# A projection stage planned with other costs and in another order, and residual sums on VectorE

## The chip, the cores and the metric

The kernel runs on one core of a Trainium2 chip. A core has five engines, each with its own queue of instructions that is worked off in order: PE (TensorE, matrix products, with PEld its weight loads), DVE (VectorE), ACT (ScalarE), POOL (GpSimd) and SP, which here only issues DMA transfers. An instruction that waits for a semaphore holds up all that stands behind it on its engine. The metric is the device time of one execution in microseconds (us), lower is better; the kernel before takes 2375.2 us, the median of three runs (2374.72 to 2376.2).

## The reference

One layer of a backbone block over 2048 latent tokens and 256 context tokens of width 1024, all in fp32:

```python
hc = modulate(rms_norm(ctx, g_pre_mix), sm_c, cm_c)
_, _, xs_c, B_c, C_c, dt_c = mixer_inputs(hc, w_in, ...)          # context: x, B, dt (C unused)
_, hf_c, hb_c = ssd_bidir(xs_c, B_c, C_c, dt_c, ..., h0, h0)      # only the final states
hx = modulate(rms_norm(x, g_pre_mix), sm_x, cm_x)
u, z, xs, B, C, dt = mixer_inputs(hx, w_in, ...)                  # p = hx @ w_in; silu(conv7(x|B|C))
y, _, _ = ssd_bidir(xs, B, C, dt, ..., hf_c, hb_c)                # chunks of 128, both directions
x = x + gm_x * rms_norm(mixer_output(u, z, xs, y, ...), g_post_mix)
hx2 = modulate(rms_norm(x, g_pre_ffn), sf_x, cf_x)
x = x + gf_x * rms_norm((silu(hx2 @ w_gate) * (hx2 @ w_up)) @ w_down, g_post_ffn)
```

`w_in` has column groups u (Fourier, 256), z (768), x (768), B (512), C (512) and dt (24); the convolution runs over 7 taps within rows of 64 latent tokens, or over the 256 context tokens as one row. `mixer_output` adds a 2-D DFT of u and ends in a product with `w_out`.

## The kernel before

Each fp32 matrix is split into a high part `hi` (cast to fp32r) and the rest `lo` (a subtraction), and a product is three matmuls: hi·hi, hi·lo and lo·hi. A weight tile of 128 columns, `raw` (512 KB), is loaded by SP, cast to `hi` by ACT (or DVE), and `lo` is made by POOL or DVE (`split`, which finish_block starts with engines by its rule `brief`; G is POOL, V DVE, S ACT, T PE).

Time runs in this order in the profiled execution: to some 105 us norms and the first z blocks; to some 690 us the rest of the projection; then 16 chunks of scan outputs and `w_out` (to 1050), FFN gate and up (to 1950), and FFN down.

**The projection.** The tokens are three sections: 2 is the context (256 columns of a matmul's output), 0 and 1 are the halves of the latent (1024 columns, two PSUM banks). A block is (kind, j, section): 128 columns of `w_in` for one section, 48 matmuls of 512 columns for a latent block and 24 of 256 for a context block, into PSUM tiles `mm` (two) or `y` in turn. The list `blocks` gives their order. A block of x, B or C is convolved from PSUM into `acc`: ACT's first term, six DVE instructions (`acc<-mm,convw,acc`, 128x1008, 992 and 976 for two each, or 255, 254 and 253 for the context), ACT's silu, and PE's transposes (`a<-ident,acc`) to token rows through the two banks `a`. z and u blocks have no taps: call them light.

All engine calls of this stage go through `Paced`, one helper line (L143), which issues the call and charges its estimated cost to a model of time, `Pace`. Work behind a block is a chain (a generator); `Pace.due` lets a chain issue its next piece between two matmul groups once PE's model time has reached the chain's due time, so the estimates set where in each engine's queue a piece stands. `drain` forces a chain out at once: at the end of a block, finish_block drains the chains of the blocks before the last. Other chains are `scan_steps` of a section (POOL and DVE), the adaLN sums (`adacc`), and `section_chain(i)`, which loads half i of section 1's tokens (`load_rows`), normalises them (`xt`), and then, once `slot_free()` holds, transposes them (`a<-ident,xt`, 32 per half) and makes the modulated hi and lo in slot C or A (`v<-a,mcs` on ACT, casts and subtractions on DVE and POOL). Section 1 starts with u0 and u1: their first halves of columns, then a drain of section_chain(1), then the second halves.

**FFN down.** The order of engines and of SP's queue here comes from the program's order through a scheduler. Two passes p of 7 positions; each position has 11 steps f of 12 matmuls (`b<-wd,hd`), weights and hidden parts for which are prepared four steps ahead (`next_w`, `down_parts`): for each step ACT casts `wd` and `hd` and DVE subtracts for their lo parts, and for some positions the weight is first a difference of blocks (`wt`, or `actC` in place). A row group's end, `finish`, scales eight tiles on DVE (`slot<-slot,rq_y,gffn`), adds the residual to each (`slot<-slot,actC`), and issues one 2 MB output transfer (`out_dram<-slot`). It is a generator too, and advances `steps(run, 2)` per f of the next position.

Of the kernel before, what the change touches and what calls it, by code (L numbers as in the profile page):

```python
# [17 lines left out]
ALU = mybir.AluOpType  # L18
# [7 lines left out]
CTX = 256  # L26
# [106 lines left out]
class Paced:  # L133
# [5 lines left out]
    def __getattr__(self, op):  # L139
        issue = getattr(self.engine, op)  # L140

        def call(out, *args, **kw):
            r = issue(out, *args, **kw)  # L143
            n = math.prod(out.shape[1:])
            if self.name == "PE":
                fp32 = op == "matmul" and args[1].dtype == F32
                n = args[1].shape[-1] if op == "matmul" else 2 * P
                cost = max(n, 64) * (4 if fp32 else 1) / 2400
            elif self.name == "ACT":
                cost = 0.19 + n * 0.00075  # L150
                table = args[1] if op == "activation" and args[1] in (AF.Silu, AF.Exp, AF.Sigmoid, AF.Ln) else None
                if table not in (None, self.table):
                    self.table, cost = table, cost + 1.3
            elif self.name == "DVE":
                cost = 0.06 + n / (1920 if op in ("tensor_scalar", "tensor_copy") else 960)
            else:
                cost = 0.15 + n * 0.0021
            self.pace.charge(self.name, cost)
            return r

        return call
# [3 lines left out]
def fourier_ssd_block(ctx, tc, a):  # L165
# [624 lines left out]
    def group(kind, sec):  # L790
        return [(kind, j, sec) for j in range({"z": ZB, "u": 2, "x": XB, "B": BB, "C": CB}[kind])]

    c_, light = group("B", 2) + group("x", 2), group("z", 0)[4:] + group("u", 0)
    blocks = group("z", 0)[:4] + [("dt", 0, 2)]
    for i, blk in enumerate(light + group("B", 0)):
        blocks += c_[i : i + 1] + [blk]
    blocks += c_[8:]
    x_ = group("x", 0)
    blocks += x_[:5] + [("dt", 0, 0)] + x_[5:] + group("C", 0)
    u_, b_, x_, z_ = group("u", 1), group("B", 1), group("x", 1), group("z", 1)  # L800
    cl = group("C", 1)
    blocks += u_ + [("dt", 0, 1)] + b_ + x_
# [6 lines left out]

    wraw, wq = {}, {}  # L810

    def want(bi):
        if bi < len(blocks) and blocks[bi][0] != "dt":
            kind, j, sec = blocks[bi]
            c0 = off[kind] + j * P
            wraw[bi] = wload(w_in[:, :, c0 : c0 + P], [P, KD, P])

    def split(bi, *engines, **where):
        if bi in wraw:
            wq[bi] = wparts(wraw.pop(bi), [P, KD, P], *engines, **where)  # L820
        yield

# [115 lines left out]
    def down_parts(p, i, f):  # L938

        hpos[1] = (7 * p + i) * ((NJ + 1) // 2) + f // 2  # L940
        hidden_loads(3 if f % 2 == 0 else 2)

        def block(b):
            return wblock[p, (b, f // 4)][:, f % 4]

        def temp():
            return ta[0].tile([P, 512], F32, tag="ws", name="wt", bufs=4)

        def sub(engine, out, x, y):
            engine.tensor_tensor(out, x, y, op=ALU.subtract)  # L950
            return out

        i_ = ORDER[p][i]
        if i_ in (1, 5):
            src = block(11)
        elif i_ in (2, 3):
            src = block({2: 21, 3: 22}[i_])
        elif i_ == 6:
            sub(G, block(11), block(12), block(11))
            src = sub(V, temp(), block(22), block(11))  # L960
        elif i_ == 7:
            src = sub(G, temp(), block(22), block(12))
        else:
            src = sub(G, temp(), block(11), block(22))
            V.tensor_tensor(src, src, block(21), op=ALU.add)
        w = wp.tile([P, 2, 512], F32R, tag=("hi", "lo")[pos[1] % 2], name="wd")
        S.copy(w[:, 0], src)
        sub(V, w[:, 1], src, w[:, 0].bitcast(F32))
        raw = hraw[7 * p + i, f // 2][:, f % 2]
        tag, bufs = (("xt", 2), ("sg", 3))[pos[1] // 2 % 2]  # L970
        h = ta[0].tile([P, 2, 512], F32R, tag=tag, name="hd", bufs=bufs)
        S.copy(h[:, 0], raw)
        sub(V, h[:, 1], raw, h[:, 0].bitcast(F32))
        return w, h
# [427 lines left out]
    with tc.manual_schedule(engines=ordered):  # L1402
# [141 lines left out]
        def settled(kinds, sec):  # L1544
            return all(b in chains and chains[b].done for b in range(2, nblk) if blocks[b][0] in kinds and blocks[b][2] == sec)

        def finish_block(bi, ps):
            kind, j, sec = blocks[bi]
            live = [chains[b] for b in plain if b in chains and not chains[b].done and (blocks[b][2] == 2) == (sec == 2)]
            pace.drain(*live[:-1])  # L1550
            two = after(bi, 2)
            brief = two < nblk and any(blocks[b][2] == 2 for b in (after(bi, 1), two))
            splits[two] = pace.start(split(two, *((V, V) if brief and blocks[two][2] != 2 else (V,) if brief else (G,))))
            chains[bi] = pace.start(column_block(kind, j, sec, ps.rearrange("p a b -> p (a b)"), lambda: read.add(bi)))
# [11 lines left out]
        while bi < nblk:  # L1566
# [9 lines left out]
            want(after(bi, 2))  # L1576
            pace.drain(splits[bi])
            pace.now = max(pace.now, splits[bi].t)
            if (kind, j, sec) == ("x", 1, 0):
                prep1[0] = pace.start(section_chain(0, lambda: True))  # L1580
            if (kind, j, sec) == ("C", 0, 0):
                pace.drain(prep1[0])
                prep1[1] = pace.start(section_chain(1, lambda: 1 in begun))
            if bi == first1:
# [10 lines left out]
                    if i == 1:  # L1595
                        finish_block(b, pz[b - bi])
                fnet = pace.start(when(lambda: settled("u", 1), fourier_steps()))
                late.append(pace.start(when(lambda: fnet.done, load_wo(0, "B"))))
                bi += 2
                continue  # L1600
            if bi == plain[-3]:
# [15 lines left out]
                pace.drain(fnet, front, wts)  # L1617
                wo1 = load_wo(1, "C")
            if after(bi, 1) == first1:
                ps = project(bi, wq.pop(bi), acts[sec], lambda: begun.update({1: True}))  # L1620
            elif bi == plain[-1]:
                ps = project(bi, wq.pop(bi), acts[sec], beside=wo1)
            else:
                ps = project(bi, wq.pop(bi), acts[sec])
            finish_block(bi, ps)
            if kind == "x" and j == XB - 1:
                scan[sec] = pace.start(when(lambda sec=sec: settled("xB", sec), scan_steps(sec)), 8.0)
            bi += 1
        fourier_split(pend[0])
        pace.window = None  # L1630
# [219 lines left out]
    def finish(p, r, o, sq):  # L1850
# [6 lines left out]
        for t in range(4):  # L1857
            for n in range(2):
                oh = o[:, t, half[n]]
                V.scalar_tensor_tensor(oh, oh, rs[0][:, t : t + 1], gffn[n], ALU.mult, ALU.mult)  # L1860
                G.tensor_tensor(oh, oh, ff.x2[:, t, half[n]], op=ALU.add)
                yield
        b = PAIRS[p][r]
        dma(out_d[4 * b * P : 4 * (b + 1) * P, :].rearrange("(t p) d -> p t d", p=P), o)
# [42 lines left out]
    def down(p, prev):  # L1907
# [3 lines left out]
        for pos_, i in enumerate(order):  # L1911
# [9 lines left out]
            while f < NJ:  # L1921
# [7 lines left out]
                for ff_ in range(f, f + m):  # L1929
                    if (pos_, ff_) in at:  # L1930
                        down_load(*at[pos_, ff_])
                    steps(run, 2)
                    if (pos_, ff_) in rows:
                        rows_load(p, rows[pos_, ff_])
                f += m
# [64 lines left out]
```

## Time and profile before

| what | value |
|---|---|
| median of three runs | 2375.2 us (2374.72 to 2376.2) |
| the profiled execution: own time | 2376.4 us |
| its span, first to last instruction | 2374.6 us |
| busy: PE, DVE, ACT, POOL | 95%, 66%, 45%, 42% of the span |
| mean granted TensorE clock | 0.984 of full speed |

A share of busy time is an average over stages; a wait of PE is what can be won. Where a view names a releaser, it is what came last before the waiting instruction could start, by the profile. A granted clock of 0.5 is the lower of two levels, 1.2 in place of 2.4 GHz.

### The profile page before, as it was taken

To read this page: it belongs to the slowest core of one execution; us is meant where nothing else is said; L and a number is where in the kernel's file an instruction comes from. 1 tells how busy PE (TensorE), PEld (TensorE's weight loads), DVE (VectorE), ACT (ScalarE), POOL (GpSimd) and SP (SyncE) were. 2 spreads that over 40 slices of the span, in tenths; PEclk is the share of its full clock that TensorE was granted. 3 is DMA by queue.
4 is the path that set the end of the run, shared out by engine and by line. 5 is a ranking of instruction groups with operands and counts; after the bars stand their busy time and mean duration, and the time that the engine had idled before them with its cause. 6 is when DMAs were issued, how large, how long until landed. Compare 5 with 4: busy or idle time off the path is not lost. (4 is left out here: it accounts for less than half of the span.)

```text
span 2374.6 us, 30049 instructions
## 1 busy us (share of the span) xinstructions
PE 2261.2 (95%) x10861; PEld 1854.2 (78%) x10861; DVE 1557.1 (66%) x2202; ACT 1079.6 (45%) x1978; POOL 999.8 (42%) x659
## 2 busy tenths in 40 slices
PE   7998998999999999988999999999999999998998
PEld 3887777777788888866888887788888878876786
DVE  3557766567557888886655556755555565779766
ACT  4433553345247777756432323332333335444454
POOL 2121526424433444434555464445454532325512
PEclk9999999999999999999999999999999999999999
DMA  9455536354687888733332332433333373547233
GB/s 308 136 161 158 160 93 227 121 157 135 195 276 219 258 252 255 245 122 116 115 102 98 103 102 93 164 111 98 111 106 102 119 268 93 195 153 255 88 124 120
DMA packets 272291, 375.02 MB, mean 158 GB/s; under 512 B 17079, under 2 KB 190211, under 8 KB 269326
## 3 DMA queue, kind: packets, MB, share of 16 engines
q1 hardware_dynamic: 242486, 342.32, 45.3%
q10 hardware_dynamic: 29656, 30.78, 3.8%
q8 instruction: 86, 1.41, 0.2%
q14 instruction: 63, 0.52, 0.1%
HBM read 278.33 MB, written 94.72 MB: 157 GB/s over the span
## 5 line engine op out<-in xcount | busy, mean ns | idle before, releaser
L143 PE MATMUL b<-wd,hd 128*128 128x512 f32 x1848 | 429.2, 394 | 16.1 <-DVE hd L143 10.8
L143 PEld LDWEIGHTS b<-wd,hd 128*128 128x128 f32 x1848 | 349.9, 190 | 95.2 <-DVE hd L143 13.4
L143 PE MATMUL mm<-slot,wa 128*128 128x512 f32 x1584 | 378.4, 392 | 10.5 <-ACT sg L143 6.9
L143 PEld LDWEIGHTS mm<-slot,wa 128*128 128x128 f32 x1584 | 297.5, 189 | 75.6 <-ACT sg L143 7.7
L143 POOL TENSOR_TENSOR ws<-raw 128x512 f32<-128x512 f32 x88 | 127.4, 1449 | 311.8 <-DMA raw<-in_w_up_dram 117.7
L143 PE MATMUL mm<-actC,wa 128*128 128x512 f32 x984 | 239.8, 392 | 7.5 <-DVE u L143 7.2
L143 PE MATMUL mm<-actB,wa 128*128 128x512 f32 x1020 | 239.3, 389 | 0.0
L143 ACT CAST wa<-ws 128x512 fp32r<-128x512 f32 x176 | 109.2, 621 | 253.2 <-PE mm L143 213.4
L143 PEld LDWEIGHTS mm<-actC,wa 128*128 128x128 f32 x984 | 185.4, 189 | 47.2 <-issue 8.8
L143 PEld LDWEIGHTS mm<-actB,wa 128*128 128x128 f32 x1020 | 191.2, 188 | 39.6
L143 DVE TENSOR_TENSOR wa<-ws,wa 128x512 fp32r<-128x512 f32 x176 | 154.4, 879 | 59.6 <-ACT wa L143 56.7
L143 PE MATMUL mm<-actA,hi 128*128 128x512 f32 x512 | 165.9, 405 | 9.6 <-DVE acc L143 6.4
L143 DVE SCALAR_TENSOR_TENSOR acc<-mm,convw,acc 128x1008 f32<-128x1008 f32 (+3 forms) x156 | 161.9, 1040 | 19.5 <-ACT acc L143 16.5
L143 POOL TENSOR_TENSOR lo<-raw,hi 128x1024 fp32r<-128x1024 f32 x34 | 81.8, 2407 | 204.4 <-ACT hi L143 200.8
L143 DVE TENSOR_TENSOR u<-u,mm 128x512 f32<-128x512 f32 x126 | 86.5, 687 | 116.4 <-PE mm L143 116.3
L143 DVE TENSOR_TENSOR wa<-raw,wa 128x512 fp32r<-128x512 f32 x132 | 120.1, 911 | 64.5 <-ACT wa L143 64.0
L143 POOL TENSOR_TENSOR rq_y<-rq_ms,mhalf 128x1 f32<-128x1 f32 (+2 forms) x60 | 41.2, 691 | 284.3 <-DVE rq_ms L143 265.8
L143 ACT CAST wa<-raw 128x512 fp32r<-128x512 f32 x132 | 82.3, 624 | 161.9 <-PE mm L143 147.3
L143 POOL TENSOR_TENSOR adacc<-adacc,adaw 128x1024 f32<-128x1024 f32 x28 | 68.3, 2439 | 136.8 <-ACT adaw L143 136.8
L143 DVE TENSOR_TENSOR hd<-hraw,hd 128x512 fp32r<-128x512 f32 x154 | 117.3, 764 | 8.3 <-ACT hd L143 8.3
L143 PEld LDWEIGHTS mm<-actA,hi 128*128 128x128 f32 x512 | 95.1, 192 | 33.2 <-DVE acc L143 6.6
L143 ACT ACTIVATE ab<-ab,lda 128x128 f32<-128x128 f32 x384 | 118.8, 391 | 0.4 <-ACT sz L143 0.4
(309 smaller groups left out, 4534.6 us busy)
## 6 DMA issues: line engine op xcount, KB each, us to landing
hraw<-hg SPq DMA_DIRECT2D x70, 512.0 KB
raw<-in_w_in_dram SPq DMA_DIRECT2D x54, 512.0 KB
ab<-acsd SPq DMA_DIRECT2D x128, 192.0 KB
raw<-in_w_gate_dram SPq DMA_DIRECT2D x44, 512.0 KB
raw<-in_w_up_dram SPq DMA_DIRECT2D x44, 512.0 KB
hg<-hs SPq DMA_DIRECT2D x22, 1024.0 KB
adaw<-in_w_ada_dram SPq DMA_DIRECT2D x32, 512.0 KB
l_x<-xtok SPq DMA_DIRECT2D x33, 384.0 KB
```

The costliest lines, as they stand in the source:

```text
L143: r = issue(out, *args, **kw)
```

## The change

1. `Paced` charges a matmul 0.0135 us more, a DVE instruction 0.02 us more, and a tap of at least 256 elements 0.2 us in place of 0.06 beside its n/960.
2. `blocks`: each of the ten B and x tiles is now taken for the context and then at once for section 0, and the latent block uses the context block's hi and lo (`shared`): ten loads of 512 KB, ten casts and ten subtractions are gone. The six light blocks z4, z5, u0, u1 (those that are left) stand behind every second pair. Then C0, C1, dt, C2, C3. Before, context blocks alternated with light blocks and B0 of section 0, and x0 to x4, dt, x5 and C0 to C3 came behind them, each with its own weights.
3. section_chain(0) starts at the last x of section 0 (was x1), section_chain(1) at C3 (was C0). A scan also waits for its section's dt, and a latent scan for the context's scan. `load_wo(0)` also waits for the adaLN sums.
4. FFN down: the residual sums and, in the second pass, 11 weight subtractions go from POOL to DVE, and finish advances one step per f in place of two.

```diff
--- before.py
+++ after.py
@@ -145,14 +145,15 @@
             if self.name == "PE":
                 fp32 = op == "matmul" and args[1].dtype == F32
                 n = args[1].shape[-1] if op == "matmul" else 2 * P
-                cost = max(n, 64) * (4 if fp32 else 1) / 2400
+                cost = max(n, 64) * (4 if fp32 else 1) / 2400 + 0.0135
             elif self.name == "ACT":
                 cost = 0.19 + n * 0.00075
                 table = args[1] if op == "activation" and args[1] in (AF.Silu, AF.Exp, AF.Sigmoid, AF.Ln) else None
                 if table not in (None, self.table):
                     self.table, cost = table, cost + 1.3
             elif self.name == "DVE":
-                cost = 0.06 + n / (1920 if op in ("tensor_scalar", "tensor_copy") else 960)
+                taps = op == "scalar_tensor_tensor" and n >= CTX
+                cost = (0.2 if taps else 0.08) + n / (1920 if op in ("tensor_scalar", "tensor_copy") else 960)
             else:
                 cost = 0.15 + n * 0.0021
             self.pace.charge(self.name, cost)
@@ -790,13 +791,12 @@
     def group(kind, sec):
         return [(kind, j, sec) for j in range({"z": ZB, "u": 2, "x": XB, "B": BB, "C": CB}[kind])]
 
-    c_, light = group("B", 2) + group("x", 2), group("z", 0)[4:] + group("u", 0)
+
+    light, cl = group("z", 0)[4:] + group("u", 0), group("C", 0)
     blocks = group("z", 0)[:4] + [("dt", 0, 2)]
-    for i, blk in enumerate(light + group("B", 0)):
-        blocks += c_[i : i + 1] + [blk]
-    blocks += c_[8:]
-    x_ = group("x", 0)
-    blocks += x_[:5] + [("dt", 0, 0)] + x_[5:] + group("C", 0)
+    for i, (kind, j, _) in enumerate(group("B", 0) + group("x", 0)):
+        blocks += [(kind, j, 2), (kind, j, 0)] + (light[i // 2 : i // 2 + 1] if i % 2 else [])
+    blocks += cl[:2] + [("dt", 0, 0)] + cl[2:]
@@ -809,14 +809,19 @@
 
     wraw, wq = {}, {}
 
+    def shared(bi):
+        return bi > 0 and blocks[bi - 1][0] != "dt" and blocks[bi] == (*blocks[bi - 1][:2], 0) and blocks[bi - 1][2] == 2
+
     def want(bi):
-        if bi < len(blocks) and blocks[bi][0] != "dt":
+        if bi < len(blocks) and blocks[bi][0] != "dt" and not shared(bi):
             kind, j, sec = blocks[bi]
             c0 = off[kind] + j * P
             wraw[bi] = wload(w_in[:, :, c0 : c0 + P], [P, KD, P])
 
     def split(bi, *engines, **where):
-        if bi in wraw:
+        if bi < len(blocks) and shared(bi):
+            wq[bi] = wq[bi - 1]
+        elif bi in wraw:
             wq[bi] = wparts(wraw.pop(bi), [P, KD, P], *engines, **where)
         yield
 
@@ -956,7 +961,7 @@
         elif i_ in (2, 3):
             src = block({2: 21, 3: 22}[i_])
         elif i_ == 6:
-            sub(G, block(11), block(12), block(11))
+            sub(V if p else G, block(11), block(12), block(11))
             src = sub(V, temp(), block(22), block(11))
         elif i_ == 7:
             src = sub(G, temp(), block(22), block(12))
@@ -1544,6 +1549,10 @@
         def settled(kinds, sec):
             return all(b in chains and chains[b].done for b in range(2, nblk) if blocks[b][0] in kinds and blocks[b][2] == sec)
 
+        def ready_to_scan(sec):
+            dt_done = any(chains[b].done for b in chains if blocks[b] == ("dt", 0, sec))
+            return settled("xB", sec) and dt_done and (sec == 2 or scan[2].done)
+
         def finish_block(bi, ps):
             kind, j, sec = blocks[bi]
             live = [chains[b] for b in plain if b in chains and not chains[b].done and (blocks[b][2] == 2) == (sec == 2)]
@@ -1576,9 +1585,9 @@
             want(after(bi, 2))
             pace.drain(splits[bi])
             pace.now = max(pace.now, splits[bi].t)
-            if (kind, j, sec) == ("x", 1, 0):
+            if (kind, j, sec) == ("x", XB - 1, 0):
                 prep1[0] = pace.start(section_chain(0, lambda: True))
-            if (kind, j, sec) == ("C", 0, 0):
+            if (kind, j, sec) == ("C", CB - 1, 0):
                 pace.drain(prep1[0])
                 prep1[1] = pace.start(section_chain(1, lambda: 1 in begun))
@@ -1595,7 +1604,7 @@
                     if i == 1:
                         finish_block(b, pz[b - bi])
                 fnet = pace.start(when(lambda: settled("u", 1), fourier_steps()))
-                late.append(pace.start(when(lambda: fnet.done, load_wo(0, "B"))))
+                late.append(pace.start(when(lambda: fnet.done and ada.done, load_wo(0, "B"))))
                 bi += 2
                 continue
             if bi == plain[-3]:
@@ -1617,14 +1626,14 @@
                 pace.drain(fnet, front, wts)
                 wo1 = load_wo(1, "C")
...
             finish_block(bi, ps)
             if kind == "x" and j == XB - 1:
-                scan[sec] = pace.start(when(lambda sec=sec: settled("xB", sec), scan_steps(sec)), 8.0)
+                scan[sec] = pace.start(when(lambda sec=sec: ready_to_scan(sec), scan_steps(sec)), 8.0)
             bi += 1
         fourier_split(pend[0])
         pace.window = None
@@ -1858,7 +1867,7 @@
             for n in range(2):
                 oh = o[:, t, half[n]]
                 V.scalar_tensor_tensor(oh, oh, rs[0][:, t : t + 1], gffn[n], ALU.mult, ALU.mult)
-                G.tensor_tensor(oh, oh, ff.x2[:, t, half[n]], op=ALU.add)
+                V.tensor_tensor(oh, oh, ff.x2[:, t, half[n]], op=ALU.add)
                 yield
         b = PAIRS[p][r]
         dma(out_d[4 * b * P : 4 * (b + 1) * P, :].rearrange("(t p) d -> p t d", p=P), o)
@@ -1929,7 +1938,7 @@
                 for ff_ in range(f, f + m):
                     if (pos_, ff_) in at:
                         down_load(*at[pos_, ff_])
-                    steps(run, 2)
+                    steps(run, 1)
                     if (pos_, ff_) in rows:
                         rows_load(p, rows[pos_, ff_])
                 f += m
```

Three places show what moved in the engines' orders. The first is DVE in FFN down, at the start of the first `finish` (wd and hd are the lo parts of a step's weights and hidden part, slot is the row group that is finished, actC the residual's rows, rq_y the row factors). Before:

```order
L143 TENSOR_SCALAR rq_ms_16823<-fss_16821 128x4
L143 TENSOR_TENSOR wd_16829<-actB_15544,wd_16829 128x512
L143 SCALAR_TENSOR_TENSOR slot_16312<-slot_16312,rq_y_16825,gffn_15361 128x512
L143 SCALAR_TENSOR_TENSOR slot_16312<-slot_16312,rq_y_16825,gffn_15362 128x512
L143 TENSOR_TENSOR hd_16854<-hraw_16710,hd_16854 128x512
```

In the changed kernel:

```order
L143 TENSOR_SCALAR rq_ms_16763<-fss_16761 128x4
L143 TENSOR_TENSOR wd_16767<-actB_15484,wd_16767 128x512
L143 TENSOR_TENSOR hd_16790<-hraw_16650,hd_16790 128x512
L143 SCALAR_TENSOR_TENSOR slot_16252<-slot_16252,rq_y_16785,gffn_15301 128x512
L143 SCALAR_TENSOR_TENSOR slot_16252<-slot_16252,rq_y_16785,gffn_15302 128x512
L143 TENSOR_TENSOR slot_16252<-slot_16252,actC_16606 128x512
L143 TENSOR_TENSOR wd_16787<-actB_15484,wd_16787 128x512
```

The sums stood in POOL's queue, eight in a row; now each pair of a scaling and a sum stands between DVE's lo parts, and the sixteen instructions spread over more steps.

The second is DVE in the projection while a context block and a latent block are worked on (hi and lo are weight parts, acc the convolved block; 16x63 is a latent tap, 255 to 253 are context taps). Before:

```order
L143 SCALAR_TENSOR_TENSOR acc<-y,convw,acc 128x255 x2
L143 SCALAR_TENSOR_TENSOR acc<-y,convw,acc 128x254 x2
L143 CAST hi<-raw 128x1024
L143 TENSOR_TENSOR lo<-raw,hi 128x1024
L143 SCALAR_TENSOR_TENSOR acc<-y,convw,acc 128x253 x2
L143 SCALAR_TENSOR_TENSOR acc<-mm,convw,acc 128x16x63
L143 TENSOR_TENSOR lo<-raw,hi 128x1024
```

In the changed kernel:

```order
L143 SCALAR_TENSOR_TENSOR acc<-mm,convw,acc 128x255 x2
L143 SCALAR_TENSOR_TENSOR acc<-mm,convw,acc 128x254 x2
L143 SCALAR_TENSOR_TENSOR acc<-mm,convw,acc 128x253 x2
L143 TENSOR_TENSOR lo<-raw,hi 128x1024
L143 SCALAR_TENSOR_TENSOR acc<-mm,convw,acc 128x16x63 x2
L143 SCALAR_TENSOR_TENSOR acc<-mm,convw,acc 128x16x62 x2
L143 SCALAR_TENSOR_TENSOR acc<-mm,convw,acc 128x16x61 x2
```

The cast of a weight tile and one of the two subtractions are gone from between the taps, so that a latent block's taps stand in one piece.

The third is PE at the start of section 1 (xt are the normalised rows of a half, actC and actA its modulated parts, xd and l_b the scan's operands). Before:

```order
L143 MATMUL mm_3088<-actC_2214,lo_2928 128x512
L143 MATMUL a_3100<-ident_81,xt_2624 128x128
L143 MATMUL a_3100<-ident_81,xt_2626 128x128
L143 MATMUL a_3100<-ident_81,xt_2628 128x128
L143 MATMUL a_3100<-ident_81,xt_2630 128x128
L143 MATMUL mm_3088<-actC_2214,hi_2926 128x512
L143 MATMUL mm_3088<-actC_2215,hi_2926 128x512
```

In the changed kernel:

```order
L143 MATMUL a_3025<-ident_81,xt_2794 128x128
L143 MATMUL a_3025<-ident_81,xt_2796 128x128
L143 MATMUL a_3025<-ident_81,xt_2798 128x128
L143 MATMUL a_3025<-ident_81,xt_2800 128x128
L143 MATMUL a_3034<-xd_2996,l_b_2959 128x192 x2
L143 MATMUL a_3038<-xd_2996,l_b_2959 128x192 x2
L143 MATMUL a_3045<-ident_81,xt_2794 128x128
L143 MATMUL a_3045<-ident_81,xt_2796 128x128
L143 MATMUL a_3045<-ident_81,xt_2798 128x128
L143 MATMUL a_3045<-ident_81,xt_2800 128x128
```

Before, groups of four transposes stood between a C or u block's matmuls; now the 32 of the second half stand behind each other, with the scan's products as the only other rows among them, ahead of the second halves of u0 and u1.

## Rows read from the trace of the kernel before

**Rows 1.** The page's first part, busy time of the engines over the span.

```profile
PE 2261.2 (95%) x10861; PEld 1854.2 (78%) x10861; DVE 1557.1 (66%) x2202; ACT 1079.6 (45%) x1978; POOL 999.8 (42%) x659
```

**Rows 2.** The table of stretches: length, then busy time (and instructions) of PE, PE's weight loads, DVE, ACT and POOL, granted clock of TensorE (1.00 is the full 2.4 GHz), DMA share, GB/s.

```profile
200.00:250.00 50.00, 42.91 (x207) 34.70 (x206) 36.05 (x42) 19.06 (x30) 9.62 (x4) 0.93 0.46 136
300.00:350.00 50.00, 45.88 (x207) 35.36 (x206) 33.57 (x42) 26.39 (x34) 14.39 (x6) 0.93 0.24 68
350.00:400.00 50.00, 43.60 (x202) 34.85 (x201) 34.81 (x40) 19.08 (x22) 33.14 (x21) 0.90 0.78 255
450.00:500.00 50.00, 43.36 (x203) 35.85 (x202) 36.51 (x50) 26.27 (x37) 20.57 (x10) 0.97 0.40 118
2100.00:2170.00 70.00, 59.56 (x245) 46.98 (x244) 63.19 (x68) 28.36 (x57) 41.96 (x26) 0.95 0.50 174
2170.00:2350.00 180.00, 177.50 (x772) 145.50 (x771) 132.41 (x186) 82.65 (x156) 56.94 (x34) 0.99 0.43 140
```

**Rows 3.** Who waited for whom, PE in 100 to 700 us: us in total, times, longest. The first and the last of eleven rows and one between; all eleven add up to 38.3 us.

```profile
PE a L143 <- ACT acc L143: 8.6, 4, 4.0
...
PE mm L143 <- DVE lo L143: 0.6, 1, 0.6
...
PE a L143 <- POOL actC L143: 0.3, 1, 0.3
```

**Rows 4.** PE's timeline: start, length, instructions, and in brackets the idle time before and its releaser. The context pairs.

```profile
212.98 0.63 PE L143 MATMUL a<-ident,acc 128*128 128x128 f32 x4 [0.72 <-DVE br L143]
...
225.79 1.22 PE L143 MATMUL mm<-actA,hi 128*128 128x512 f32 x2 [6.37 <-DVE acc L143]
```

**Rows 5.** PE's timeline further on: four waits, and two rows of matmuls at the full clock behind the last of them.

```profile
269.47 1.12 PE L143 MATMUL a<-ident,xt 128*128 128x128 f32 x8 [2.37 <-DVE h L143]
...
330.96 1.14 PE L143 MATMUL a<-dtp,kc 128*128 128x96 f32 x4 [4.12 <-DVE dtp L143]
...
392.95 1.65 PE L143 MATMUL a<-xd,l_b 128*128 128x192 f32 x4 [6.35 <-ACT v L143]
...
490.60 1.70 PE L143 MATMUL a<-ident,acc 128*128 128x128 f32 x8 [4.01 <-ACT acc L143]
...
495.21 0.62 PE L143 MATMUL mm<-actC,hi 128*128 128x512 f32 x2
495.66 0.39 PE L143 MATMUL mm<-actC,lo 128*128 128x512 f32 x1
```

**Rows 6.** The table of stretches again (columns as in rows 2), two windows of 10 us.

```profile
170.00:180.00 10.00, 10.00 (x47) 8.31 (x46) 9.70 (x12) 2.66 (x4) 2.40 (x1) 1.00 0.60 164
220.00:230.00 10.00, 4.21 (x12) 3.43 (x13) 9.61 (x14) 2.85 (x4) 2.17 (x1) 0.73 0.61 176
```

**Rows 7.** PE in FFN down: two rows of who waited for whom (us, times, longest) in 1950 to 2374 us, and one of its timeline.

```profile
PE b L143 <- DVE hd L143: 10.1, 5, 4.0
PE b L143 <- DVE wd L143: 1.8, 1, 1.8
...
2127.46 27.79 PE L143 MATMUL b<-wd,hd 128*128 128x512 f32 x120 [1.67 <-DVE hd L143]
```

**Rows 8.** The timeline of DVE in FFN down, and one row of POOL's (the residual sums).

```profile
2119.23 1.78 DVE L143 TENSOR_TENSOR wd<-actB,wd 128x512 fp32r<-128x512 f32 x1
...
2122.63 1.40 DVE L143 SCALAR_TENSOR_TENSOR slot<-slot,rq_y,gffn 128x512 f32<-128x512 f32 x2
...
2127.93 0.68 DVE L143 TENSOR_TENSOR wd<-slot,wd 128x512 fp32r<-128x512 f32 x1
2128.53 0.68 DVE L143 TENSOR_TENSOR hd<-hraw,hd 128x512 fp32r<-128x512 f32 x1
...
2117.02 5.13 POOL L143 TENSOR_TENSOR slot<-slot,actC 128x512 f32<-128x512 f32 x3 [0.62 <-DVE slot L143]
```

**Rows 9.** The issue of an output transfer on SP's queue, and ACT's first evacuation of PSUM into a buffer of the same pool behind it.

```profile
2168.81 0.55 SPq L1864 DMA_DIRECT2D out_dram<-slot  x1
...
2177.71 0.59 ACT L143 COPY slot<-b 128x512 f32<-128x512 f32 x1 [0.27 <-PE b L143]
```

**Rows 10.** DVE's groups of instructions in 100 to 700 us, shapes apart: xcount, busy us, mean ns of one, idle before.

```profile
L143 DVE SCALAR_TENSOR_TENSOR acc<-mm,convw,acc 128x1008 f32<-128x1008 f32 x38 | 47.9, 1261 | 16.8 <-ACT acc L143 16.5
...
L143 DVE TENSOR_TENSOR lo<-raw,hi 128x1024 fp32r<-128x1024 f32 x16 | 21.6, 1351 | 10.2 <-ACT hi L143 9.3
...
L143 DVE CAST hi<-raw 128x1024 fp32r<-128x1024 f32 x8 | 9.2, 1150 | 24.7 <-PE mm L143 16.5 <-PE y L143 8.2
...
L143 DVE TENSOR_SCALAR xt<-xt,rq_y 128x1024 f32<-128x1024 f32 x8 | 7.6, 987 | 0.0
L143 DVE CAST actA<-v 128x512 fp32r<-128x512 f32 x8 | 6.8, 855 | 8.8 <-ACT v L143 8.8
L143 DVE SCALAR_TENSOR_TENSOR acc<-mm,convw,acc 128x254 f32<-128x254 f32 x14 | 6.7, 482 | 0.4
...
L143 DVE TENSOR_TENSOR actA<-v,actA 128x512 fp32r<-128x512 f32 x4 | 3.9, 981 | 0.2
```

**Rows 11.** The same view for ACT.

```profile
L143 ACT ACTIVATE acc<-acc 128x1024 f32<-128x1024 f32 x28 | 29.6, 1057 | 63.7 <-DVE acc L143 63.7
L143 ACT ACTIVATE acc<-mm,vcol,convw 128x1024 f32<-128x1024 f32 x19 | 22.8, 1202 | 2.4 <-PE mm L143 2.4
...
L143 ACT ACTIVATE v<-a,mcs 128x512 f32<-128x512 f32 x16 | 12.2, 777 | 20.3 <-PE a L143 17.5 <-POOL actA L143 1.9 <-DVE actA L143 0.7
```

More of the change, by code (lines that the diff above doesn't have):

```diff
@@ L1619, in fourier_ssd_block @@
             if after(bi, 1) == first1:
-                ps = project(bi, wq.pop(bi), acts[sec], lambda: begun.update({1: True}))
+                ps = project(bi, wq[bi], acts[sec], lambda: begun.update({1: True}))
             elif bi == plain[-1]:
-                ps = project(bi, wq.pop(bi), acts[sec], beside=wo1)
+                ps = project(bi, wq[bi], acts[sec], beside=wo1)
             else:
-                ps = project(bi, wq.pop(bi), acts[sec])
+                ps = project(bi, wq[bi], acts[sec])
             finish_block(bi, ps)
             if kind == "x" and j == XB - 1:
-                scan[sec] = pace.start(when(lambda sec=sec: settled("xB", sec), scan_steps(sec)), 8.0)
+                scan[sec] = pace.start(when(lambda sec=sec: ready_to_scan(sec), scan_steps(sec)), 8.0)
             bi += 1
```

## The prediction

> **What bounds the kernel now.** I read the page's engine totals first. PE is busy 2261.2 of 2374.6 us [rows 1], so all that any edit outside PE's own work can win is its 113.4 us of idle time and what a halved clock costs. In 700 to 1950 us the changed kernel has PE's instructions in the same order, one for one, and nearly all of the other engines' too; I take that part as unchanged. The table of stretches came next, for the rest [rows 2]. The change can act in 100 to 700 (the projection) and 2100 to 2350 (FFN down).
>
> In the projection the view of who waited for whom adds up to 38.3 us of PE waiting [rows 3]. The granted clock adds to it: a stretch of 50 us at 0.93 did 3.5 us less work than at 1.00, so 200–250, 300–350, 350–400 and 450–500 lost 3.5 + 3.5 + 5.0 + 1.5 = 13.5 us [rows 2]. Each of the four follows a long wait (6.37, 4.12, 6.35 and 4.01 us [rows 4, 5]): the matmuls right behind such a wait run at the lower of the two levels (two in 1.22 us at 225.79, against 0.62 at 495.21 [rows 4, 5]). A wait that goes takes its dip along. Together 51.8 us could come back.
>
> The waits differ by place. In 120–260 DVE is the limit: 9.70 of 10 us busy in 170–180, 9.61 in 220–230 while PE does 4.21 [rows 6]. Around the other waits DVE has 33 to 37 of 50 us [rows 2], and PE waits because a short instruction stood behind long ones in an in-order queue.
>
> In FFN down six waits, five on hd and one on wd, make 10.1 + 1.8 = 11.9 us [rows 7], and the clock adds 0.05 x 70 = 3.5 and 0.01 x 180 = 1.8 [rows 2]: 17.2. They coincide with the residual sums on POOL. DVE's subtraction of two SBUF operands starts every 0.60 us when POOL rests (2127.93, 2128.53), and takes 1.78 when a sum lies beside it (three sums in 5.13, 1.71 each) [rows 8]. So each sum costs DVE about 1.1 us. The Trainium skill ("SBUF — State Buffer", section "Who interferes with whom") says that a two-input VectorE instruction and a GpSimd one that reads SBUF exclude each other for a whole instruction; 1.78 against 0.60 agrees.
>
> **FFN down.** 24 sums leave POOL for DVE and 11 subtractions of the second pass too, and finish takes one step per f, not two. Per sum DVE loses a 1.1 us blockage and gains 0.60 us. Is there room? In the first of the places shown from the engines' orders, DVE's 28 rows from the first scaling to the last sum are 8 scalings at 0.66 (two in 1.40, the next begins 1.32 on [rows 8]) and 20 two-input rows at 0.60: 17.3 us. Six f's of PE are 6 x 2.78 = 16.7 (120 matmuls in 27.79 us, 12 per f [rows 7]). DVE falls back 0.6 us against a lead of up to three f's: no wait, but at full load. In the next finish 39 rows, 31 x 0.60 + 8 x 0.66 = 23.9 us, stand against nine f's, 25.0. The 11 moved subtractions make four two-input rows per f, 2.4 of 2.78. The out transfer now leaves near the end of a position, one position before its buffer gets new results from ACT; before, issue to that copy was 2168.8 to 2177.7 [rows 9], at most 8.9 us, against three prepared f's of 8.3. Against the move speaks the Trainium skill ("Perfetto Trace Analysis", section "Optimizing Scalar/DVE Operations"): when VectorE is saturated, offload work from it. By that rule this would lose; the same section warns that the two engines share a port, and the 1.78 us of the trace shows that here the offload itself costs more than the work. Bounds: 0 (blockage gone, DVE full instead) to 17.2. I take 13, nearer the top, since the load reaches 100% only in the first finish.
>
> **Context pairs (120–285).** Before, a pair of a context block and the next one cost DVE six taps of 1.25 (7.5), six of 0.48 (2.9), and for two weight tiles a cast of 1.15 and subtractions of 1.35 [rows 10]. With the latent block's cast and subtraction both there that is 7.5 + 2.9 + 2 x 1.35 + 1.15 = 14.2 against PE's 13.5: 48 x 0.225 = 10.8 (two matmuls begin 0.45 before the next, at 495.21 and 495.66 [rows 5]) and for the context 24 of half the columns, 2.7. DVE cannot keep up. Afterwards one tile serves both: 7.5 + 2.9 + 1.35 = 11.8, and behind every second pair stands a light block of 10.8 us of PE with no DVE work but a split. DVE's load is 2 x 11.8 + 1.35 = 24.9 of 2 x 13.5 + 10.8 = 37.8 us. The ten dropped loads, ACT casts and subtractions lie beside PE and give nothing else. What goes: 0.55 + 0.72 + 6.37 of waits [rows 3, 4] and 3.5 of clock: 11.1. What is late next is the transposes of a latent block, placed some 12 to 15 us behind its matmuls; six taps and two activations (7.5 + 1.2 + 1.1 [rows 10, 11]) need 9.8. Bounds 3 (the 6.37 halves only) to 11.1; I take 10.
>
> **C blocks, dt and the start of section 1 (285–410).** Here I expect a loss. Before: 2.37 + 0.33 + 4.12 + 6.35 = 13.2 of waits [rows 3, 5] and 8.5 of clock. Section_chain(0) starts four blocks later, so its 32 transposes share two PSUM banks with scan 2 in the one block C1: eight hand-overs of about 0.78 (one ACT evacuation [rows 11]), 6 us (bounds 2.7, as before, to 12). dt: 3.5 (3 to 4.1). Section_chain(1) starts at C3 where it started at C0; its 32 transposes now stand in one piece after u1's first half (the third of the places shown). PE waits there for the scaled rows (four times 0.99 on DVE [rows 10], behind taps), then for eight hand-overs of which its own 0.60 us transposes cover part: 9.5 (bounds 3.5, ACT's 8 x 0.78 less 8 x 0.60 and 2 for the rows, to 14). Dips 7.7 (5 to 9). Sum 26.7 against 21.7: −5, bounds +7 to −17.
>
> **Section 1 (410–690).** The rest of the 38.3 us, 38.3 − 7.6 − 13.2 = 17.5, and 1.5 of clock [rows 2, 3]. Before, taps were charged 0.06 + n/960 (1.11 us for 1008) where they take 1.26, and a matmul 0.213 where it takes 0.225; the planner's DVE thus ran about 1 us per block ahead of the real one, and a block's transposes went out at the block boundaries, in the forced drain. With 1.25 and 0.227 charged, they stand in mid-block with 3 to 5 us of slack by my sum of rows over PE's order. I keep 4 of waits, so 15 could go; bounds 0 to 19. I take 12, since scan and Fourier also move.
>
> **Sum.** −13 − 10 + 5 − 12 = −30 from the profiled execution's own 2376.4: 2346.4. The runs' median is 2375.2, 1.2 less: 2345.
>
> **Rivals.** (a) Everything found comes back: 17.2 + 11.1 + 15 and C to u1 as before, −43: 2332. For it: DVE has room on paper in each stretch. Against: hand-overs of two banks. (b) Only FFN down and the context pairs give; section 1's waits move to other places, C to u1 loses 5 to 10: −13 − 10 + 8 = −15: 2360. For it: ten separate small waits in section 1 with five different releasers, which better taps alone need not cure. (c) It does not do what it says: the planner's waits move, and DVE at full load in FFN down replaces the blockage: within 5 of 2375. Against: the 6.37 us has its own cause, removed. (d) Slower: the modulation of section 1's second half. It is one forced drain with nothing else for PE; each of eight groups goes transposes, ACT, cast, subtraction (0.60 + 0.78 + 0.86 + 0.98 = 3.2 us [rows 10, 11]), and if the groups go one after the other, behind the C blocks' taps on DVE (3 blocks of 7.5), it is 26 + 15 = 41 us, in place of 9.5, with a dip: +32 against −30 of the rest, 2380. It decides from 30 us of waiting at that place on. Against it: two banks and three engines overlap, and before the same chain cost 6.35.
>
> **How the numbers follow.** Forecast 0.52, own range 2336 to 2355; (a) 0.15; (b) 0.18; (c) 0.07; (d) 0.08. All lower bounds of time together give 17.2 + 11.1 + 7 + 19 = −54, all upper ones 0 − 3 + 17 − 0 = +14; neither is likely at once. Range for 8 in 10: 2327 (past (a)) to 2367 (past (b)). About 0.2%, 4.8 us, is what a measurement of this kernel can tell from no change. Faster by more: 0.52 + 0.15 + 0.18 and a little of (c), 0.87; within: 0.05; slower: 0.08.
>
> **What would show it.** FFN down: in 2100–2190 no DVE row of 1.7 us beside POOL and under 3 us of PE waits; wrong if DVE is 10.0 of 10 over 30 us with waits on wd or hd. Context pairs: no wait on acc over 2 us before 285 and DVE under 8.5 of 10. C to u1: one wait of 4 to 14 us before the second halves, releaser ACT v or DVE, and some on "a" banks in C1; over 30 us means (d). Section 1: waits on acc under 4 us in sum. The forecast as a whole is wrong if the clock dips are as many as before.

## The result, and the profile after

The changed kernel takes 2356.6 us (four runs, 2355.1 to 2359.9) against 2375.6, the median of four runs of the kernel before that were taken beside it: a ratio of 0.9922, 95% interval 0.9905 to 0.9939, some 19 us faster. The forecast was 2345, so −30. The profiled execution is the slowest of the four, with a span of 2358.1 us.

Where the 19 us come from is seen by the starts of two late stages. The rows are PE's first matmuls of FFN gate and of FFN down, first in the kernel before:

```profile
1036.45 2.88 PE L143 MATMUL mm<-slot,wa 128*128 128x512 f32 x12
...
1919.62 8.32 PE L143 MATMUL b<-wd,hd 128*128 128x512 f32 x36
```

and in the changed kernel:

```profile
1035.78 2.88 PE L143 MATMUL mm<-slot,wa 128*128 128x512 f32 x12
...
1921.25 8.32 PE L143 MATMUL b<-wd,hd 128*128 128x512 f32 x36
```

Gate starts 0.7 us earlier, down 1.6 us later. FFN down to the span's end took 2374.6 − 1919.6 = 455.0 us before and 2358.1 − 1921.3 = 436.8 after: 18.2 us less. All that lies ahead of it won nothing that two profiles can tell apart (the experiments show how far such starts scatter). The table of stretches (columns as in rows 2) shows that this nothing is a sum. Before:

```profile
100.00:285.00 185.00, 174.66 (x908) 146.79 (x908) 126.55 (x166) 75.11 (x103) 48.23 (x24) 0.98 0.51 152
285.00:410.00 125.00, 114.47 (x526) 91.14 (x525) 87.68 (x102) 52.16 (x63) 55.99 (x32) 0.93 0.52 165
410.00:700.00 290.00, 272.45 (x1348) 224.45 (x1348) 180.60 (x248) 120.98 (x169) 121.00 (x61) 0.99 0.57 181
```

After:

```profile
100.00:285.00 185.00, 184.73 (x954) 155.65 (x954) 106.89 (x134) 75.10 (x97) 40.87 (x17) 1.00 0.45 134
285.00:410.00 125.00, 105.32 (x465) 80.86 (x464) 81.47 (x108) 54.71 (x71) 52.10 (x30) 0.89 0.43 136
410.00:700.00 290.00, 275.38 (x1370) 228.14 (x1369) 189.85 (x254) 121.51 (x167) 130.29 (x67) 0.98 0.58 187
2100.00:2180.00 80.00, 80.00 (x353) 65.95 (x352) 74.79 (x126) 40.37 (x78) 3.72 (x3) 1.00 0.70 241
```

In 100 to 285 PE goes from 174.66 to 184.73 us of 185 at the full clock; [rows 4] have no counterpart left. In 285 to 410 it loses: 114.47 to 105.32, and the clock falls from 0.93 to 0.89. In 410 to 700 it gains 3 us of busy time and loses 0.01 of clock on 290. Over the three together PE is busy 565.4 us in place of 561.6, but the low clock costs 13.8 + 5.8 = 19.6 us (the part lacking to 1.00 times the length, stretch by stretch) where it cost 3.7 + 8.8 + 2.9 = 15.4. In 2100 to 2180 the waits of [rows 7] are gone, 80.00 of 80. Who waited for whom, PE in 100 to 700 us, shows what stands there in place of [rows 3]:

```profile
PE a L143 <- DVE h L143: 13.8, 2, 10.2
PE a L143 <- ACT v L143: 4.6, 4, 2.4
PE a L143 <- DVE dtp L143: 4.2, 1, 4.2
...
PE a L143 <- ACT acc L143: 1.0, 1, 1.0
```

All eleven rows add up to 34.1 us where [rows 3] had 38.3. The waits on acc have shrunk from 8.6 us to 1.0; one on `h`, the scan's state, is the longest now.

DVE's timeline in the first finish answers to [rows 8]:

```profile
2111.80 1.41 DVE L143 SCALAR_TENSOR_TENSOR slot<-slot,rq_y,gffn 128x512 f32<-128x512 f32 x2
2113.12 0.68 DVE L143 TENSOR_TENSOR slot<-slot,actC 128x512 f32<-128x512 f32 x1
2113.72 0.68 DVE L143 TENSOR_TENSOR wd<-actB,wd 128x512 fp32r<-128x512 f32 x1
2114.33 0.68 DVE L143 TENSOR_TENSOR slot<-slot,actC 128x512 f32<-128x512 f32 x1
```

Sums (`slot<-slot,actC`) and lo parts start 0.60 us apart, and none takes 1.78. In the second finish DVE has no idle time over 20 us, and PE (first column) does not wait. The kernel before has DVE at 10.00 of 10 in both windows too, but with 9 and 7 rows done where there are now 18 and 17, and PE busy for 5.93 and 5.99 us:

```profile
2150.00:2160.00 10.00, 10.00 (x46) 8.29 (x45) 10.00 (x18) 4.53 (x8) 0.00 (x0) 1.00 0.64 197
2160.00:2170.00 10.00, 10.00 (x45) 8.29 (x45) 10.00 (x17) 5.79 (x12) 0.00 (x0) 1.00 0.63 220
```

### The profile page after: what moved, and what is told of

Its sections match the earlier page's. It is cut to its first block, busy times and chain, and to the rows that moved or that the text cites. A ratio compares the mean times of both kernels' runs of the same rounds, so it can differ in the third digit from the quotient of the medians.

```text
span 2358.1 us, 29985 instructions
## 1 busy us (share of the span) xinstructions
PE 2261.0 (96%) x10861; PEld 1855.0 (79%) x10861; DVE 1531.9 (65%) x2220; ACT 1082.5 (46%) x1979; POOL 943.3 (40%) x623
## 5 line engine op out<-in xcount | busy, mean ns | idle before, releaser
L143 PE MATMUL b<-wd,hd 128*128 128x512 f32 x1848 | 423.0, 391 | 4.2 <-ACT hd L143 2.0
L143 DVE TENSOR_TENSOR hd<-hraw,hd 128x512 fp32r<-128x512 f32 x154 | 109.9, 714 | 5.7 <-ACT hd L143 5.6
```

## The experiments

All are timed beside the kernel before on the same chip (medians of 2374.8 to 2375.4 us); ratios are to it. The first four are about FFN down and the sum of the two halves of the change, the others about the projection. A profile of one run has its limits here: before, e1, e3 and e4 have the same instructions ahead of FFN down, and their first gate matmul starts at 1036.5, 1034.2, 1033.4 and 1035.7 us; the changed kernel and e2, which share theirs, have 1035.8 and 1033.8. Differences of 3 us between two profiles of that part are not read.

**e1_down_only.** The kernel before with part 4 of the change:

```diff
-                G.tensor_tensor(oh, oh, ff.x2[:, t, half[n]], op=ALU.add)
+                V.tensor_tensor(oh, oh, ff.x2[:, t, half[n]], op=ALU.add)
-                    steps(run, 2)
+                    steps(run, 1)
-            sub(G, block(11), block(12), block(11))
+            sub(V if p else G, block(11), block(12), block(11))
```

> The kernel before with part 4 of the change alone (sums and the second pass's subtractions on DVE, finish one step per f). Theory one, FFN down gives all of the gain: 2357 to 2359 us, the waits on hd and wd in FFN down under 3 us in sum, the projection as before. Theory two, the gain needs both halves of the change: 2366 or more.

Measured: 2357.0 us, 0.9931 (0.9916 to 0.9946). Who waited for whom, PE in 1950 to 2374 us, has for `b` only this left:

```profile
PE b L143 <- DVE slot L143: 1.4, 3, 0.7
```

Theory one: this part alone gives 18.0 us, nearly as much as the whole change's 19.

**e2_proj_only.** The changed kernel with the three edits above undone.

> The changed kernel with part 4 undone: new costs, order, sharing and chain starts, FFN down as before. Theory one (context pairs win some 12 us, the start of section 1 and the blocks behind it give all of it back): 2373 to 2376 us, FFN down with 11 to 12 us of waits on hd and wd again. Theory two: 2366 or less, the projection gives half of the gain.

Measured: 2377.0 us, 1.0007 (0.9998 to 1.0016), a little above the range named. The projection's edits as they stand are worth nothing, and the same view shows FFN down's waits as in [rows 7]:

```profile
PE b L143 <- DVE hd L143: 9.7, 5, 3.5
PE b L143 <- DVE wd L143: 1.8, 2, 1.5
```

**e3_sums_fast** has only the first of the three edits, **e4_steps_only** only the second.

> The kernel before with the residual sums on DVE, but two steps of finish per f and the subtractions on POOL. If the engine of the sums is what counts: 2358 to 2362 us. If the slower pace of finish is needed too, since DVE then has 4 of 6 two-input rows per f too many (about 3.6 us of DVE work per f of 2.78): 2364 to 2370, with waits of PE on hd and wd of 5 to 8 us left.

> The kernel before with one step of finish per f and the sums still on POOL. If the blockage itself is the cause, spreading halves its density and most of the lost DVE time is caught up by the three prepared steps: 2360 to 2366 us. If each blockage costs PE time whatever its spacing: 2372 to 2376.

Measured: e3 2361.8 us, 0.9951 (0.9934 to 0.9967); e4 2371.2 us, 0.9987 (0.9977 to 0.9996). The engine of the sums brings 13.1 us, the rest of part 4 another 4.8 (by medians; the intervals of e1 and e3 overlap). In e3 two waits in the second finish are left (PE's timeline), where two steps per f ask DVE for more than a step's time (by the estimate above, 3.6 us of 2.78):

```profile
2153.83 3.01 PE L143 MATMUL b<-wd,hd 128*128 128x512 f32 x12 [1.71 <-DVE hd L143]
2158.59 6.64 PE L143 MATMUL b<-wd,hd 128*128 128x512 f32 x28 [1.75 <-DVE hd L143]
```

In e4 the waits remain at nearly their size, though the sums are spread out (who waited for whom, PE in 1950 to 2374 us):

```profile
PE b L143 <- DVE hd L143: 5.3, 3, 2.3
PE b L143 <- DVE wd L143: 4.0, 1, 4.0
```

e4 lies between its two cases and nearer to the second: spacing gives 3.7 us, the blockage by POOL is what costs. Whether the slower pace or the moved subtractions bring e1's last 4.8 us was not tried apart.

**e5_prep_early** starts section_chain(1) one block sooner.

```diff
-            if (kind, j, sec) == ("C", CB - 1, 0):
+            if (kind, j, sec) == ("C", CB - 2, 0):
```

> The changed kernel (2356.6 us) with section_chain(1) started at C2 in place of C3. Theory one, its rows come too late (PE waits on xt, 2.33 and 0.34 us at 385 us, and the four waits behind them): those on xt go, 2350 to 2354 us. Rival, the hand-overs of the two banks in the drained piece are the price, whenever the rows are there: 2355 to 2358.

Measured: 2359.4 us, 0.9932 (0.9918 to 0.9947). The waits on xt went, but others stand in PE's timeline, one of them on POOL's weight split. The first and the last row are the start of u0 and of its second half:

```profile
369.52 0.61 PE L143 MATMUL mm<-actC,hi 128*128 128x512 f32 x2
...
377.79 0.50 PE L143 MATMUL mm<-actC,lo 128*128 128x512 f32 x1 [1.70 <-POOL lo L143]
...
388.19 1.58 PE L143 MATMUL a<-ident,xt 128*128 128x128 f32 x8 [1.97 <-ACT v L143]
391.90 1.62 PE L143 MATMUL a<-xd,l_b 128*128 128x192 f32 x4 [2.14 <-issue]
...
396.39 1.20 PE L143 MATMUL mm<-actA,hi 128*128 128x512 f32 x2
```

By time this is the rival's case, and 1 us above it; by mechanism it is neither. The stretch from the start of u0 to that of its second half is shorter, 26.9 us (396.39 − 369.52) where the changed kernel takes 33.8 (its rows stand below), and its waits are 7.1 us in place of 8.8. The gain is lost behind it: in 410 to 700 PE is busy 271.6 us where it was 275.4, and gate starts at 1036.1.

**e6_old_costs** and **e8_no_sharing** take the new estimates, or the sharing, out of the changed kernel.

```diff
-        return bi > 0 and blocks[bi - 1][0] != "dt" and ...
+        return False and bi > 0 and blocks[bi - 1][0] != "dt" and ...
```

> The changed kernel with the estimates of the kernel before, order and sharing kept. If the new estimates are worth something: 2360 to 2367 us, with waits on acc back in section 1 (410 to 700 us). If they are worth nothing in this order: 2354 to 2359.

> The changed kernel with a load and a split of its own for every block, order kept. If sharing is what removes the wait on DVE in the context pairs (14.2 us of DVE work against 13.5 of PE per pair without it): 2361 to 2368 us with waits on acc or lo before 300 us. If the light blocks between the pairs give room enough: 2355 to 2359 and no such wait.

Measured: e6 2352.3 us, 0.9906 (0.9891 to 0.9921); e8 2349.2 us, 0.9890 (0.9875 to 0.9904). Both are faster than the changed kernel, which neither theory had. In e6 the waits on acc are back, as forecast, with 7.4 us in 410 to 700, and still it is 4.3 us faster. In e8 every block splits its own weights again, and yet (the table of stretches, 100 to 285 and 170 to 180 us):

```profile
100.00:285.00 185.00, 184.73 (x955) 155.84 (x954) 124.94 (x157) 76.53 (x99) 40.66 (x17) 1.00 0.53 156
170.00:180.00 10.00, 10.00 (x57) 8.75 (x56) 7.61 (x7) 2.93 (x3) 2.41 (x1) 1.00 0.80 243
```

PE waits for nothing there, with DVE at 7.61 of 10 where [rows 6] have 9.70. Sharing is not what removed the wait of 6.37 us, and the new estimates are not either: f2 below, with neither, is busy 184.39 of 185 there, and f3, with the new estimates in the old order, keeps a wait of 6.51 on acc at 226.23. It is the order; that the light blocks between the pairs give DVE the room is the reading that fits.

**e7_fourier_after_scan** holds one chain back.

```diff
-                fnet = pace.start(when(lambda: settled("u", 1), fourier_steps()))
+                fnet = pace.start(when(lambda: settled("u", 1) and scan[0].done, fourier_steps()))
```

> The changed kernel with the Fourier chain held until the scan of section 0 is done. Theory one, PE's wait of 10.16 us at 478 us is the scan's h addition standing on DVE behind Fourier's pieces (5.58 us for four of them beside POOL): it goes with the low clock behind it, 2343 to 2350 us. Rival, DVE is full there in any order (scan, taps and dt together) and the wait only moves: 2354 to 2360.

Measured: 2355.5 us, 0.9920 (0.9903 to 0.9936), the rival's range. PE's wait of 10.16 us is gone from the trace, so that Fourier stood in the way holds; but PE's timeline has a new one close by, for section 1's dt:

```profile
449.02 1.14 PE L143 MATMUL a<-dtp,kc 128*128 128x96 f32 x4 [5.50 <-DVE dtp L143]
```

In DVE's timeline ahead of it, seven short pieces of dt take 8.61 us; another takes 0.36 at 447.07, when POOL rests:

```profile
438.26 8.61 DVE L143 SCALAR_TENSOR_TENSOR dtp<-dtp 128x192 f32<-128x192 f32 x7
```

In that time POOL runs four rows with two inputs each, from 437.51 to 445.48 without a gap.

**f1_noshare_fourier** is e7 and e8 in one, **f2_order_alone** is e6 and e8 in one, **f4_noshare_fourier_old** all three. **f3_costs_down** is e1 with the new estimates: the old order, no sharing.

> The changed kernel without sharing and with the Fourier chain held until section 0's scan is done, both edits together. If each removes a wait of its own (sharing: the start of section 1; Fourier: the wait behind the scan at 450 to 490 us): 2341 to 2346 us. If both only draw another arrangement of the same queue pieces, their gains don't add: 2347 to 2356.

> The changed kernel without sharing and with the old estimates: of the projection's edits the order, the chain starts and the scan's conditions alone. If order is what gives in the projection, and estimates and sharing nothing: 2346 to 2353 us, PE without a wait from 100 to 300 us. If sharing or estimates were needed for it: 2356 or more.

> The kernel before with part 4 (2357.0 us without more) and the new estimates, old order and no sharing. If the estimates mend the waits of section 1, as forecast: 2342 to 2350 us. If they only move them: 2353 to 2361.

> No sharing, Fourier held, old estimates, with the changed order and part 4. If the old estimates gain 4 us in any arrangement, as they seemed to in the first: 2338 to 2344 us. If estimates only draw another arrangement: 2345 to 2354.

Measured, with the other kernels that have part 4:

| order | sharing | Fourier held | old estimates | new estimates |
|---|---|---|---|---|
| old | no | no | e1: 2357.0 | f3: 2347.0, 0.9882 (0.9869 to 0.9896) |
| new | no | no | f2: 2363.9, 0.9955 (0.9942 to 0.9967) | e8: 2349.2 |
| new | no | yes | f4: 2351.1, 0.9900 (0.9886 to 0.9913) | f1: 2343.9, 0.9872 (0.9857 to 0.9887) |
| new | yes | no | e6: 2352.3 | the changed kernel: 2356.6 |
| new | yes | yes | not run | e7: 2355.5 |

The new estimates are worth 10.0, 14.7 and 7.2 us in the first three rows, and cost 4.3 in the fourth. Sharing gains 11.6 us with the old estimates and loses 7.4 with the new (11.6 with Fourier held). The new order with its chain starts and scan conditions alone loses 6.9 us, or 2.2 with the new estimates. Holding Fourier gives 12.8, 5.2 or 1.1. So no edit of the projection has a value of its own. f1 lies in the range of its first case and f3 too, f2 and f4 in that of their second. f1's first case holds by time alone: the two gains by themselves are 7.4 and 1.1 us, together they are 12.7. Why the edits act on each other like this is not shown.

A few rows show something of how. In f2, PE's waits in 410 to 700 us on acc (the convolved block) are back; e8, the same order with the new estimates, has 1.1:

```profile
PE a L143 <- ACT acc L143: 12.9, 4, 5.2
```

In f3 PE's busy time in two of the stretches shown above is 118.05 and 281.76 us, 3.6 and 9.3 more than before, and the clock in the first is 0.97 in place of 0.93 (in 100 to 285 it is 4.1 less):

```profile
285.00:410.00 125.00, 118.05 (x557) 94.17 (x558) 91.54 (x107) 55.58 (x67) 59.13 (x32) 0.97 0.58 178
410.00:700.00 290.00, 281.76 (x1400) 233.46 (x1399) 184.39 (x255) 127.04 (x183) 116.06 (x59) 0.99 0.57 183
```

f1 is the fastest of all, 31 us under the kernel before and 13 under the changed one.

## Why the prediction was right, and where it was not

The sign, the range and FFN down as the largest piece were right, but FFN down gave all of it. The forecast had the projection at −17 (−10 + 5 − 12), and e2 has it at about 0 (1.0007); the range of 8 in 10 held because FFN down gave 5 us more than forecast and the range was wide. That part is luck. The sign that the prediction named for being wrong as a whole, as many clock dips as before, did come: in 100 to 700 us they cost 19.6 us where they had cost 15.4, and the mean clock of the profiled execution is 0.984 as before. By its steps:

**FFN down, −13.** Measured −18.0 (e1), a little more than the bound of 17.2. The mechanism was the one named: DVE blocked beside POOL's sums. What made me keep 4 us back, DVE at full load, cost PE nothing over 20 us at 10.00 of 10; that the prepared steps carried it is the likely reason. It came in the second finish, which the sum had at 23.9 of 25.0 us, and not in the first. The feared output transfer did no harm: no wait of FFN down names it. The Trainium skill ("Perfetto Trace Analysis", section "Optimizing Scalar/DVE Operations") says only that offloading from a saturated VectorE, even to GpSimd, may make sense, and that between these two it might not help, since they share a port. e3, 13.1 us faster with the sums on VectorE, agrees with the second.

**Context pairs, −10.** All the waits named went, and u0 starts 12.4 us earlier (rows below). But "DVE cannot keep up" was wrong as a reason for sharing: I set 14.2 us of DVE against one pair's 13.5 of PE, while the new order puts a light block of 10.8 behind every two pairs. With 14.2 in both pairs and 1.35 for the light block that is 29.8 us of 37.8, and e8 has no wait there. The mean of 1.15 us for a cast that I used [rows 10] also held blocked rows, which the last section shows.

**C blocks to u1, +5.** Mis-sized: it is some +10. The waits were near the forecast, 19.4 us in sum where 19 were named: 6.4 around scan 2 (6), 4.2 for dt (3.5) and 8.8 between the start of u0 and that of its second half (9.5). But these 8.8 are nine short waits and not one, the longest 2.45, and the clock over the stretch cost (1 − 0.89) x 125 = 13.8 us where I put 7.7. From the first matmul of u0 to the first on actA, which is the start of its second half, the changed kernel takes 33.8 us (405.17 − 371.39; the longest of the nine waits between):

```profile
371.39 0.62 PE L143 MATMUL mm<-actC,hi 128*128 128x512 f32 x2
...
397.33 1.65 PE L143 MATMUL a<-xd,l_b 128*128 128x192 f32 x4 [2.45 <-ACT v L143]
...
405.17 1.31 PE L143 MATMUL mm<-actA,hi 128*128 128x512 f32 x2
```

and the kernel before 23.8 (407.62 − 383.78):

```profile
383.78 0.71 PE L143 MATMUL mm<-actC,hi 128*128 128x512 f32 x2
...
407.62 0.75 PE L143 MATMUL mm<-actA,hi 128*128 128x512 f32 x2
```

So u0 started 12.4 us earlier than before, and its second half 2.5. Not all of the 10 us between is lost: 24 of the 32 transposes stood ahead of u0 before. In the profiles of e5, e8 and e6 the same piece takes 26.9, 26.1 and 27.3 us. What in the queues makes it so much shorter there is open, and e5 shows that a shorter piece alone does not make the kernel faster.

**Section 1, −12.** This term failed: the second halves start 2.5 us earlier than before and gate 0.7, so it came out at about nothing (+2, less than profiles of that part scatter). The waits on acc did shrink, as forecast. What I had set aside with "scan and Fourier also move" took their place. With dt and the chain of section 0 later, its scan now falls into section 1's first blocks together with Fourier's pieces and section 1's dt. PE's longest wait of the projection stands there. The rows are PE's, then DVE's and POOL's around it:

```profile
477.82 2.50 PE L143 MATMUL a<-kc,actB 128*128 128x128 f32 x10 [10.16 <-DVE h L143]
...
467.13 5.58 DVE L143 SCALAR_TENSOR_TENSOR actB<-va 128x128 f32<-128x128 f32 x4
...
475.48 0.48 DVE L143 SCALAR_TENSOR_TENSOR actB<-va 128x128 f32<-128x128 f32 x2
...
477.23 1.01 DVE L143 TENSOR_TENSOR h<-h,a 128x384 f32<-128x384 f32 x2
...
466.94 1.60 POOL L143 TENSOR_TENSOR h<-h,hdec 128x768 f32<-128x768 f32 x1
468.50 2.38 POOL L143 TENSOR_TENSOR adacc<-adacc,adaw 128x1024 f32<-128x1024 f32 x1
470.84 1.51 POOL L143 TENSOR_TENSOR xd<-l_x,scs 128x768 f32<-128x768 f32 x1
```

PE needs a bank of `a` that DVE's `h<-h,a` empties at 477.23. Ahead of that in DVE's queue stand taps, dt and four pieces of Fourier (`actB<-va`, two SBUF inputs) that take 5.58 us while POOL runs three long rows with SBUF operands. Two more take 0.48 at 475.48. In the kernel before, four of them took 1.63; there too a POOL row reached into the first, to 461.50, and the other three took 0.28 each (DVE's row, then POOL's):

```profile
460.63 1.63 DVE L143 SCALAR_TENSOR_TENSOR actB<-va 128x128 f32<-128x128 f32 x4 [1.40 <-ACT va L143]
...
458.97 2.53 POOL L143 TENSOR_TENSOR lo<-raw,hi 128x1024 fp32r<-128x1024 f32 x1 [3.87 <-ACT hi L143]
```

It looks like the blockage of FFN down over again, in a place to which the change had moved it. e7 bears this out and shows its limit: without Fourier there, it is dt's pieces that POOL's rows stretch, and 1.1 us is won. The term's own reason, that measured durations put transposes where they don't wait, holds in the new order: the waits on acc go from 12.9 us in f2 to 1.1 in e8, and from 7.4 in e6 to 1.0 in the changed kernel. But its price does not follow from them, for the first pair gains 14.7 us and the second loses 4.3. In the old order the new estimates gain 10.0 us and those waits stay (who waited for whom, PE in 410 to 700 us, e1 and then f3):

```profile
PE a L143 <- ACT acc L143: 6.9, 3, 4.0
...
PE a L143 <- ACT acc L143: 7.1, 3, 3.7
```

**The rivals.** By time it ended between the forecast's own range and (b), 2360; (b)'s mechanism, "section 1's waits move to other places, C to u1 loses 5 to 10", is what happened. (d), 41 us of waiting at the drained piece, did not happen: PE waits 8.8 there, far under the 30 that were to decide it. Its sum was wrong too, since three blocks of 7.5 are 22.5 and not 15. (c) held for the projection alone: e2 at 1.0007.

## What to carry to other kernels

Ask of each engine that gets an "offloaded" elementwise operation what it does to the other one while it runs: here a POOL sum of 1.7 us cost DVE 1.1 us, more than the 0.60 us of doing it there. When a planner's estimates, order and inputs change together, time each alone and in pairs: in the new order estimates alone were worth 14.7 us and sharing alone 11.6, both together 7.3. A stage that ends where it began can hide a gain of 12 us in its first part; compare the start of the next stage as well as the waits.

## What was not expected of the hardware

POOL blocks a DVE instruction with one SBUF input as well. In the timeline of the kernel before, DVE's cast of a weight tile takes 0.69 us where no POOL row runs as it begins, and 1.91 in three of its eight rows there, each of which starts 1.04 or 1.05 us after a POOL row of some 2.40 that has two SBUF inputs (DVE's rows, then POOL's):

```profile
122.84 0.69 DVE L143 CAST hi<-raw 128x1024 fp32r<-128x1024 f32 x1 [4.05 <-PE mm L143]
...
137.73 1.91 DVE L143 CAST hi<-raw 128x1024 fp32r<-128x1024 f32 x1 [6.62 <-PE mm L143]
...
136.69 2.40 POOL L143 TENSOR_TENSOR adacc<-adacc,adaw 128x1024 f32<-128x1024 f32 x1 [10.89 <-ACT adaw L143]
```

The row ends 0.55 us after POOL's at 139.09, so the cast seems to have run once POOL was done. The Trainium skill ("SBUF — State Buffer", section "Who interferes with whom") has it so: a cast can enter a mode that uses the port pair shared with GpSimd. In f3 POOL's rows of this stretch lie elsewhere, all eight casts take about 0.69 us, and the mean is 694 ns against 1150 in [rows 10].
